# First projection of a hybrid decoder layer: a fixed row-by-row order, one low half on GpSimd, and VectorE's low parts as scalar_tensor_tensor

## The chip, the cores and the metric

The kernel runs on one core of a Trainium2 chip. The metric is the time of one execution in microseconds (us) on the device; lower is better. The core has five engines that run side by side, each working through its own list of instructions in order: TensorE (PE in the profile, with weight loads as PEld), VectorE (DVE), ScalarE (ACT), GpSimd (POOL) and SyncE (SP, which here only starts transfers). They meet through semaphores. Transfers between the memory outside (HBM) and the on-chip memory SBUF are done by 16 DMA engines.

## The reference, cut to what matters

One decoder layer with 256 tokens of width 2048. The part that the change touches is the beginning: a modulated RMS norm and the first projection.

```python
c_act = jax.nn.silu(c)
mod = (c_act @ w_ada[l] + b_ada[l]).reshape(B, 6, 1, D)
shift1, scale1, gate1, shift2, scale2, gate2 = jnp.moveaxis(mod, 1, 0)
h = rmsnorm(x, g_norm_mix[l]) * (1.0 + scale1) + shift1
q_a, k_c, v_c, k_s, v_s, k_w, v_w, g_a, q_r, k_r, v_r, g_r = split_cols(h @ w_in[l], IN_SIZES)
...
x = x + gate1 * (jnp.concatenate([o_nsa, o_ret], axis=-1) @ w_out[l])
h2 = rmsnorm(x, g_norm_ffn[l]) * (1.0 + scale2) + shift2
x = x + gate2 * peer_ffn(h2, peer_w_q[l], peer_sub_keys[l], peer_u[l], peer_v[l])
return rmsnorm(x, g_norm_final)
```

Everything is float32. Behind the projection come sparse attention, retention, the output projection and a retrieval over 16,384 experts; the change leaves them alone.

## The kernel before, in words

**Products in two parts.** TensorE multiplies in a shortened float32 format. To keep the precision, each operand is split: `hi` is the value rounded to that format (a cast on ScalarE), `lo` is the rest, `value - hi` (a subtraction on VectorE). A product is then three matmuls: hi·hi, hi·lo and lo·hi. `split` (L157, L158) makes `whi` and `wlo` of a weight tile `raw` (128 partitions x 2048 columns, 1,024 KB) in two halves of 1024 columns: cast, subtract, cast, subtract.

**The first projection, stage A.** It runs over eight rows k of `winA` (the first eight of the 16 blocks of 128 input features; 2048 output columns). Per row: SP starts the load of `winA[k]` (L348); `split` makes its parts; `row_in(k)` makes the activations of the block with `modulate`: ScalarE scales and shifts the block of `xT` (L295) and casts it to `hh` (L296), VectorE writes the low part `hl` (L297; `hh` and `hl` are the two halves of the tile `act`); TensorE runs 48 matmuls of 128x256 into eight PSUM banks, `bkA` (L354): first hi·hi for the first block of each bank, then the rest, bank by bank.

**Scales and shifts row by row.** The scale and shift of a block come from two rows of `w_ada`, which is read alongside as 128x2048 tiles, `adaT`. `ada_chunk` (L198) multiplies such a tile with the row `crow` and adds up over the columns, one VectorE instruction of 128x2048 and a small one that reads the accumulator out. `background` takes these tiles off a list; a row of stage A takes two (scale and shift of the next row) and then writes `modc` (L338) and `scol` (L339), which ScalarE needs for the next row's L295. So a row loads three tiles of 1,024 KB: one `winA`, two `adaT`.

**Buffers.** The raw tiles rotate through four buffers. SP starts loads in the order of the code, and a load waits until its buffer's last reader is done. `whi` and `wlo` have two buffers each.

**Before and behind stage A.** Ahead of it the squares of `xT` are summed, GpSimd raises the mean to the power -1/2 (L221), TensorE spreads it over the partitions, ScalarE copies it out (`rrow`, L275), and VectorE multiplies `xT` with it in four instructions (L300). Behind it the eight banks are copied out to `oT`, by VectorE and ScalarE in turn (L370, L372, `wait_in`), and stage C follows with four tiles `winC` of the same shape into the banks `bkC`, then stage B with 16 rows of `winB` (832 KB each).

**What sets the order.** The order on each engine is chosen by a scheduler from an estimate of times; only what is passed to `tc.keep_in_program_order` stays in the order of the code among such instructions of its engine. In stage A nothing was held in this way.

Of the kernel before, what the change touches and what calls it, by code (L numbers as in the profile page):

```python
# [9 lines left out]
F32 = mybir.dt.float32  # L10
F32R = mybir.dt.float32r
# [5 lines left out]
AF = mybir.ActivationFunctionType  # L17
OP = mybir.AluOpType
# [97 lines left out]
def body(ctx, tc, a, out, dbg=None, stop=None):  # L116
    nc = tc.nc
# [15 lines left out]
    def chunk_tile(name, dt, tag=None):  # L133
        pool, bufs = strm[-1]
        return pool.tile([P, 2048], dt, name=name, tag=tag or name, bufs=bufs[tag or name])
# [10 lines left out]
    def load(src):  # L146
        r = raw_tile()
        i = nc.sync.dma_start(r, src)
        if ring:
            tc.keep_in_program_order(i)  # L150
        return r

    def split_to(r, hi, lo, parts=1):
        n = hi.shape[-1] // parts
        for i in range(parts):
            sl = slice(i * n, i * n + n)
            nc.scalar.copy(hi[:, sl], r[:, sl])  # L157
            nc.vector.tensor_sub(lo[:, sl], r[:, sl], hi[:, sl].bitcast(F32))  # L158

    def split(r, n=2048, parts=2):  # L160
        hi, lo = chunk_tile("whi", F32R)[:, 0:n], chunk_tile("wlo", F32R)[:, 0:n]
        split_to(r[:, 0:n], hi, lo, parts)
        return hi, lo
# [4 lines left out]
    xT = base.tile([P, KB, S], F32, name="xT")  # L168
# [3 lines left out]
    b_col = cols[:, 0:96].rearrange("p (j k) -> p j k", k=KB)  # L172
    g_mix, g_ffn = cols[:, 96:112], cols[:, 112:128]
# [3 lines left out]
    modc = base.tile([P, 6, KB], F32, name="modc")  # L177
    scol = base.tile([P, 2, KB], F32, name="scol")
    def c_row(pool, psum=None, dst=None):

        r = pool.tile([P, D], F32, name="crow") if dst is None else dst
        if psum is None:
            nc.sync.dma_start(r, bass.AP(tensor=a["c"].tensor, offset=a["c"].offset, ap=[[0, P], [1, D]]))
            nc.scalar.activation(r, r, AF.Silu)
            return r
        c1 = raw_tile()[0:1, :]
        nc.sync.dma_start(c1, a["c"])
        for q in range(4):
            sl = slice(q * 512, (q + 1) * 512)
            ps = psum.tile([P, 512], F32, name="psc_", tag="A")  # L190
            nc.tensor.matmul(ps, ones[0:1, :], c1[:, sl], start=True, stop=True)
            nc.scalar.activation(r[:, sl], ps, AF.Silu)
        return r

    def ada_chunk(j, k, crow):

        r = load(a["adaT"][j, k])
        nc.vector.scalar_tensor_tensor(r, r, 1.0, crow, op0=OP.mult, op1=OP.mult, accum_out=modc[:, j, k:k + 1])  # L198

    def gate_store(j, ps, ident, t):  # L200

# [24 lines left out]
    hh, hl = act[:, :, 0, :], act[:, :, 1, :]  # L226
# [52 lines left out]
    with ExitStack() as fctx:  # L279
# [12 lines left out]
        def modulate(k, e, t, gi, sh, hh, hl):  # L292

            for i in range(k, e):
                nc.scalar.activation(t[:, i - k, :], t[:, i - k, :], AF.Identity, bias=modc[:, sh, i:i + 1], scale=scol[:, gi, i:i + 1])  # L295
            nc.scalar.copy(hh[:, k:e, :], t)  # L296
            nc.vector.tensor_sub(hl[:, k:e, :], t, hh[:, k:e, :].bitcast(F32))  # L297
# [14 lines left out]
        crow = c_row(fp, pp)  # L312
# [11 lines left out]
        todo = [(j, k) for k in range(KB) for j in (1, 0)] + [(j, k) for j in (2, 4, 3) for k in range(KB)] + [(5, k) for k in range(LATE)]  # L324

        credit = [0.0]

        def background(n=1):
            credit[0] += PACE[n] if isinstance(n, str) else n
            n = int(credit[0] + 1e-6)  # L330
            credit[0] -= n
            for _ in range(n):
                if not todo:
                    return
                j, k = todo.pop(0)
                ada_chunk(j, k, crow)
                if j == 0:
                    nc.vector.tensor_add(modc[:, 0:2, k], modc[:, 0:2, k], b_col[:, 0:2, k])  # L338
                    nc.vector.tensor_scalar(scol[:, 0, k:k + 1], modc[:, 1, k:k + 1], 1.0, g_mix[:, k:k + 1],  # L339
                                            op0=OP.add, op1=OP.mult)  # L340
                elif 1 < j < 5 and k == KB - 1:
                    nc.vector.tensor_add(modc[:, j, :], modc[:, j, :], b_col[:, j, :])
                    if j == 4:
                        nc.vector.scalar_tensor_tensor(scol[:, 1, :], modc[:, 4, :], 1.0, g_ffn, op0=OP.add, op1=OP.mult)

        def win_row(src, k, n):
            r = raw_tile()
            nc.sync.dma_start(r[:, 0:n], src[k])  # L348
            return split(r, n)

        def rows_T(bank, b, hi, lo, col, k, k0, k1, first=True):
            w = slice(col, col + P)
            for n, (x, y) in enumerate(((hi, hh), (hi, hl), (lo, hh))):
                nc.tensor.matmul(bank[:, b, :], x[:, w], y[:, k, :], start=k == k0 and n == 0 and first,  # L354
                                 stop=k == k1 - 1 and n == 2, skip_group_check=True)
# [6 lines left out]
        def row_in(k):  # L362
            while len(todo) > 80 + LATE - 2 * (k + 1):
                background(1)
            modulate(k, k + 1, xT[:, k:k + 1, :], 0, 0, hh, hl)

        def wait_in(dst, bk):
            for i, b in enumerate(bk):
                if i % 2:
                    nc.vector.tensor_copy(dst[:, 2 * i:2 * i + 2, :], b)  # L370
                else:
                    nc.scalar.copy(dst[:, 2 * i:2 * i + 2, :], b)  # L372

        background(2)
        bk = banks("bkA", [P, 2, S], "AASSTTOO")
        for k in range(KH):
            hi, lo = win_row(a["winA"], k, 2048)
            row_in(k)
            background("A")
            for b in range(16):  # L380
                rows_T(bk[b // 2], b % 2, hi, lo, b * P, k, 0, KH, b % 2 == 0)
        wait_in(oT, bk)
        bk = banks("bkC", [P, 2, S], "AASS")
        for q in range(KH // 2):
            hi, lo = split(load(a["winC"][q].rearrange("p k e -> p (k e)")))
# [8 lines left out]
        for k in range(KB):  # L394
            hi, lo = win_row(a["winB"], k, NB)
# [80 lines left out]
        for kv in range(2):  # L476
# [9 lines left out]
            for pb in range(16):  # L486
                i = nc.tensor.matmul(psc, w1[:, pb * P:(pb + 1) * P], blk[:, pb], start=pb == 0, stop=pb == 15)
# [34 lines left out]
        for gp in range(2):  # L522
# [3 lines left out]
            for r in range(4):  # L526
# [5 lines left out]
                for hf in range(2):  # L532
# [5 lines left out]
                    for br in range(2):  # L538
# [6 lines left out]
                        for tt, sl in ((0, slice(0, 128)), (1, slice(128, 384))):  # L545
# [3 lines left out]
                                                 accum_out=den[:, hf, tt, br:br + 1])  # L549
# [155 lines left out]
        for q in range(4):  # L705
            sl = slice(q * 512, (q + 1) * 512)
# [9 lines left out]
            with tc.high_priority(offset=100 if q == 3 else 0):  # L716
                for tt in range(2):
                    t = fp.tile([P, 512], F32, name="xg", tag="tmp2", bufs=3)
# [8 lines left out]
        for q in range(4):  # L727
            sl = slice(q * 512, (q + 1) * 512)
# [3 lines left out]
        for k in range(KB):  # L732
            with tc.high_priority(offset=(KB - k) * 10):
# [3 lines left out]
                t = xT[:, k, :]  # L737
# [9 lines left out]
    with ExitStack() as gctx:  # L747
# [49 lines left out]
        pin = tc.keep_in_program_order  # L797
# [544 lines left out]
def build(tc, a, out, dbg=None):  # L1342
    with ExitStack() as ctx:
        body(ctx, tc, a, out, dbg)
# [17 lines left out]
```

## Time and profile before

| | us |
|---|---|
| three runs, median | 1861.81 (1858.59 to 1864.34) |
| the profiled execution | 1856.91 |
| its span, first to last instruction | 1855.2 |
| TensorE busy in the span | 1793.1 (97%) |
| VectorE busy | 1485.7 (80%) |
| ScalarE busy | 708.7 (38%) |
| GpSimd busy | 366.1 (20%) |

How to read the lines that the prediction quotes. In the chain of waits a piece has its start and length in us and then what the time went to: an engine's line and tile, or a transfer. In the windows a line is a stretch of the span with each engine's busy time and its number of instructions. A row of the timeline has start, length, engine, line, operation, the tiles written and read, their shapes, the number of merged instructions, and in brackets how long the engine had been idle and what ended the wait. A row of a group of instructions has the busy time in us and the mean of one in ns. "adaT multiply" stands for L198, "low half" for L158 on 1024 columns.

### The profile page before, as it was taken

Reading aid. Unit: us, or ns where it says so; the run is one execution under the profiler, and the core shown is the slowest. Engines: PE = TensorE matmul, PEld = TensorE weight load, DVE = VectorE, ACT = ScalarE, POOL = GpSimd, SP = SyncE. Lnnn points to the kernel's source line nnn. Section 1 sums busy time; section 2 is a strip of 40 time slices with the busy share of each in tenths; the row PEclk is TensorE's granted clock in tenths of the full one; section 3 lists DMA queues with packets and bytes.
Section 4 is the critical chain, followed back from the end, with each engine's and each line's share of the span. In section 5 each row is a group of like instructions: output and inputs, shape, how many; then the busy total and the mean of one; then the engine's idle time right before and its main releaser. Section 6 shows DMA issues by size and latency. Waiting matters only on the chain.

```text
span 1855.2 us, 28510 instructions
## 1 busy us (share of the span) xinstructions
PE 1793.1 (97%) x11264; PEld 1571.5 (85%) x11264; DVE 1485.7 (80%) x2336; ACT 708.7 (38%) x1284; POOL 366.1 (20%) x259
## 2 busy tenths in 40 slices
PE   5899999999889999999999999999999999999997
PEld 4899878797767899999997777779999998777775
DVE  7988889889779999586498999983555558998878
ACT  3444453745435421021045555541111114555554
POOL 1000001011010012211124434420111114544210
PEclk9999899999999999999999999999999999999999
DMA  8989887889887799999889999989999989999992
GB/s 341 409 320 362 313 308 292 342 302 334 318 338 279 278 322 364 424 366 376 332 346 386 423 420 416 409 355 425 367 345 359 354 316 404 426 421 403 388 316 99
DMA packets 94616, 653.96 MB, mean 353 GB/s; under 512 B 11409, under 2 KB 11633, under 8 KB 18449
## 3 DMA queue, kind: packets, MB, share of 16 engines
q1 hardware_dynamic: 66818, 467.78, 65.2%
q0 software_dynamic: 27664, 184.37, 25.3%
q8 instruction: 88, 1.44, 0.3%
q14 instruction: 46, 0.38, 0.1%
HBM read 644.97 MB, written 4.22 MB: 350 GB/s over the span
## 4 chain that ended last, share of the span: by engine, by line
PE 87%; DVE 7%; DMA 3%; issue 1%; ACT 1%; POOL 0%; SPq 0%; ACTq 0%; POOLq 0%; DVEq 0%
PE acc L990 31%; PE psU L1111 28%; PE psN L453 8%; PE psD L354 4%; PE psA L237 3%; PE bkB L354 2%; DMA raw<-in_adaT 2%; PE psA L238 1%; PE pg L1096 1%; DVE raw L198 1%; DVE wlo L158 1%; PE bkC L354 1%; PE bvB L406 1%; DMA raw<-in_winA 1%; PE pT L552 1%
## 5 line engine op out<-in xcount | busy, mean ns | idle before, releaser
L1111 PE MATMUL psU<-xT,raw 128*128 128x160 f32 x4096 | 569.5, 300 | 0.0
L1111 PEld LDWEIGHTS psU<-xT,raw 128*128 128x128 f32 x4096 | 558.3, 190 | 0.4
L990 PE MATMUL acc<-whi,cc 128*128 128x512 f32 x1512 | 369.1, 391 | 0.0
L990 PEld LDWEIGHTS acc<-whi,cc 128*128 128x128 f32 x1512 | 283.8, 188 | 70.0 <-issue 1.5
L967 DVE TENSOR_TENSOR wlo<-raw,whi 128x2048 fp32r<-128x2048 f32 x126 | 288.1, 2287 | 55.1 <-issue 47.4
L990 PE MATMUL acc<-wlo,cc 128*128 128x512 f32 x1008 | 254.2, 392 | 0.8 <-DVE wlo L967 0.6
L964 ACT CAST whi<-raw 128x2048 fp32r<-128x2048 f32 x126 | 240.7, 1911 | 0.5 <-DMA raw<-in_v 0.5
L198 DVE SCALAR_TENSOR_TENSOR raw<-raw,crow 128x2048 f32<-128x2048 f32 x96 | 219.0, 2283 | 19.7 <-DMA raw<-in_adaT 19.6
L157 ACT CAST whi<-raw 128x1024 fp32r<-128x1024 f32 (+1 forms) x174 | 168.5, 1018 | 167.1 <-DMA raw<-in_winA 32.4
L158 DVE TENSOR_TENSOR wlo<-raw,whi 128x1024 fp32r<-128x1024 f32 (+1 forms) x174 | 200.6, 1181 | 24.2 <-ACT whi L157 23.8
L990 PEld LDWEIGHTS acc<-wlo,cc 128*128 128x128 f32 x1008 | 161.5, 161 | 63.8 <-DVE wlo L967 3.1
L453 PE MATMUL psN<-whi,act 128*128 128x512 f32 x512 | 166.9, 402 | 1.4 <-ACT act L677 0.7
L1117 DVE TENSOR_TENSOR X<-X,ge 128x160 f32<-128x160 f32 (+19 forms) x94 | 25.8, 276 | 162.7 <-ACT ge L1116 160.5
L1113 ACT ACTIVATE X<-psU 128x160 f32<-128x160 f32 (+19 forms) x102 | 25.6, 251 | 315.6 <-PE psU L1111 299.6
L453 PEld LDWEIGHTS psN<-whi,act 128*128 128x128 f32 x512 | 95.9, 189 | 25.6 <-issue 1.7
L453 PE MATMUL psN<-wlo,act 128*128 128x512 f32 x256 | 103.3, 404 | 3.4 <-DVE wlo L158 3.4
L953 ACT CAST cc<-X 128x192 fp32r<-128x192 f32 x126 | 44.0, 352 | 148.1 <-PE acc L990 147.5
L237 PE MATMUL psA<-act,whi 128*128 128x512 f32 x240 | 87.2, 404 | 3.8 <-ACT whi L157 3.8
L806 POOL DMA_INDIRECT rows<-in_urow,sx x32 | 67.1, 2097 | 105.3 <-DVE rows L847 100.4
L806 POOL DMA_INDIRECT s<-in_urow,sx x26 | 53.9, 2072 | 120.6 <-DVE s L847 86.5
L354 PE MATMUL psD<-act,whi 128*128 128x256 f32 x384 | 75.4, 294 | 0.6 <-ACT whi L157 0.6
L969 ACT CAST cc<-cc 128x64 fp32r<-128x64 f32 x126 | 30.4, 243 | 117.2 <-DVE cc L954 117.2
(363 smaller groups left out, 2551.0 us busy)
## 6 DMA issues: line engine op xcount, KB each, us to landing
raw<-in_u SPq DMA_DIRECT2D x128, 1024.0 KB
raw<-in_v SPq DMA_DIRECT2D x128, 1024.0 KB
raw<-in_adaT SPq DMA_DIRECT2D x96, 1024.0 KB
raw<-in_winN SPq DMA_DIRECT2D x16, 1024.0 KB
raw<-in_woutN SPq DMA_DIRECT2D x16, 1024.0 KB
raw<-in_wqT SPq DMA_DIRECT2D x16, 1024.0 KB
raw<-in_winB SPq DMA_DIRECT2D x16, 832.0 KB
raw<-in_winD SPq DMA_DIRECT2D x12, 1024.0 KB
```

Of the source, the lines that this page charges most:

```text
L157: nc.scalar.copy(hi[:, sl], r[:, sl])
L158: nc.vector.tensor_sub(lo[:, sl], r[:, sl], hi[:, sl].bitcast(F32))
L198: nc.vector.scalar_tensor_tensor(r, r, 1.0, crow, op0=OP.mult, op1=OP.mult, accum_out=modc[:, j, k:k + 1])
L237: nc.tensor.matmul(p_, hi[:, sl], act[:, k], start=k == 0, stop=False, skip_group_check=True)
L354: nc.tensor.matmul(bank[:, b, :], x[:, w], y[:, k, :], start=k == k0 and n == 0 and first, stop=k == k1 - 1 and n == 2, skip_group_check=True)
L453: nc.tensor.matmul(ps[tt], x[:, k, ts_], y[:, w], start=k == 0 and j == 0, stop=k == KB - 1 and j == 2)
L806: pin(nc.gpsimd.indirect_dma_start(out=r, out_offset=None, in_=src, in_offset=bass.IndirectOffsetOnAxis(ap=o, axis=0)))
L953: inorder(nc.scalar.copy(ch, xb(j)))
L964: inorder(nc.scalar.copy(hi, r))
L967: nc.vector.tensor_sub(lo[:, i:i + n], r[:, i:i + n], hi[:, i:i + n].bitcast(F32))
L990: return nc.tensor.matmul(acc[c][0:m], x, w[:, c[1] * 512:(c[1] + 1) * 512], start=jj == 0 and n == 0, stop=jj == HALF - 1 and n == 2 - c[ ...
L1111: nc.tensor.matmul(ps, w[:, k * P:(k + 1) * P], xT[:, k, 0:TU], start=k == 0, stop=k == KB - 1)
```

## The change

In stage A alone (a flag, `pinned`, is set ahead of its loop and cleared behind it):

- Every instruction of a row on ScalarE, VectorE and GpSimd is held in the order of the code, row by row: casts and low halves of the weights, activation, its cast and its low part, then the two adaT multiplies of the next row with `modc` and `scol`.
- The second low half of each `winA` tile is subtracted on GpSimd (L367 of the new code), the first one stays on VectorE.
- VectorE's subtractions of the stage (first low half and low part of the activations, both L353) are written as `scalar_tensor_tensor`, (x * 1.0) - y, in place of `tensor_sub`.

```diff
     def ada_chunk(j, k, crow):
 
         r = load(a["adaT"][j, k])
-        nc.vector.scalar_tensor_tensor(r, r, 1.0, crow, op0=OP.mult, op1=OP.mult, accum_out=modc[:, j, k:k + 1])
+        return nc.vector.scalar_tensor_tensor(r, r, 1.0, crow, op0=OP.mult, op1=OP.mult, accum_out=modc[:, j, k:k + 1])
...
         credit = [0.0]
+        pinned = [False]
+
+        def pin(i):
+            return tc.keep_in_program_order(i) if pinned[0] else i
...
                 j, k = todo.pop(0)
-                ada_chunk(j, k, crow)
+                pin(ada_chunk(j, k, crow))
                 if j == 0:
-                    nc.vector.tensor_add(modc[:, 0:2, k], modc[:, 0:2, k], b_col[:, 0:2, k])
-                    nc.vector.tensor_scalar(scol[:, 0, k:k + 1], modc[:, 1, k:k + 1], 1.0, g_mix[:, k:k + 1],
-                                            op0=OP.add, op1=OP.mult)
+                    pin(nc.vector.tensor_add(modc[:, 0:2, k], modc[:, 0:2, k], b_col[:, 0:2, k]))
+                    pin(nc.vector.tensor_scalar(scol[:, 0, k:k + 1], modc[:, 1, k:k + 1], 1.0, g_mix[:, k:k + 1],
+                                                op0=OP.add, op1=OP.mult))
...
+        def minus(dst, x, y):
+            if pinned[0]:
+                pin(nc.vector.scalar_tensor_tensor(dst, x, 1.0, y, op0=OP.mult, op1=OP.subtract))
+            else:
+                nc.vector.tensor_sub(dst, x, y)
+
         def win_row(src, k, n):
             r = raw_tile()
             nc.sync.dma_start(r[:, 0:n], src[k])
-            return split(r, n)
+            if not pinned[0]:
+                return split(r, n)
+            hi, lo = chunk_tile("whi", F32R)[:, 0:n], chunk_tile("wlo", F32R)[:, 0:n]
+            for i in range(2):
+                sl = slice(i * n // 2, (i + 1) * n // 2)
+                pin(nc.scalar.copy(hi[:, sl], r[:, sl]))
+                if i:
+                    pin(nc.gpsimd.tensor_sub(lo[:, sl], r[:, sl], hi[:, sl].bitcast(F32)))
+                else:
+                    minus(lo[:, sl], r[:, sl], hi[:, sl].bitcast(F32))
+            return hi, lo
...
         def row_in(k):
             while len(todo) > 80 + LATE - 2 * (k + 1):
                 background(1)
-            modulate(k, k + 1, xT[:, k:k + 1, :], 0, 0, hh, hl)
+            t = xT[:, k:k + 1, :]
+            pin(nc.scalar.activation(t[:, 0, :], t[:, 0, :], AF.Identity, bias=modc[:, 0, k:k + 1], scale=scol[:, 0, k:k + 1]))
+            pin(nc.scalar.copy(hh[:, k:k + 1, :], t))
+            minus(hl[:, k:k + 1, :], t, hh[:, k:k + 1, :].bitcast(F32))
...
         bk = banks("bkA", [P, 2, S], "AASSTTOO")
+        pinned[0] = True
         for k in range(KH):
             hi, lo = win_row(a["winA"], k, 2048)
             row_in(k)
             background("A")
             for b in range(16):
                 rows_T(bk[b // 2], b % 2, hi, lo, b * P, k, 0, KH, b % 2 == 0)
+        pinned[0] = False
```

What it does to the order. On VectorE, from the end of the norm's small instructions to row 1 (`wlo<-raw,whi` are low halves, `xT<-xT,rrow` is the normalisation, `act<-xT,act` the low part of the activations, `raw,modc<-raw,crow` an adaT multiply) the kernel before has:

```order
L269 TENSOR_SCALAR rdiag<-small,rcol 128x128 x2
L158 TENSOR_TENSOR wlo<-raw,whi 128x1024 x2
L300 TENSOR_TENSOR xT<-xT,rrow 128x1024 x4
L198 SCALAR_TENSOR_TENSOR raw,modc<-raw,crow 128x2048
L297 TENSOR_TENSOR act<-xT,act 128x256
L198 SCALAR_TENSOR_TENSOR raw,modc<-raw,crow 128x2048
L158 TENSOR_TENSOR wlo<-raw,whi 128x1024
L338 TENSOR_TENSOR modc<-modc,cols 128x2
L158 TENSOR_TENSOR wlo<-raw,whi 128x1024
L198 SCALAR_TENSOR_TENSOR raw,modc<-raw,crow 128x2048
L339 TENSOR_SCALAR scol<-modc,cols 128x1
L198 SCALAR_TENSOR_TENSOR raw,modc<-raw,crow 128x2048
```

and the changed kernel, on the same engine at the same place:

```order
L269 TENSOR_SCALAR rdiag<-small,rcol 128x128 x2
L300 TENSOR_TENSOR xT<-xT,rrow 128x1024 x4
L353 SCALAR_TENSOR_TENSOR wlo<-raw,whi 128x1024
L353 SCALAR_TENSOR_TENSOR act<-xT,act 128x256
L198 SCALAR_TENSOR_TENSOR raw,modc<-raw,crow 128x2048 x2
L343 TENSOR_TENSOR modc<-modc,cols 128x2
L344 TENSOR_SCALAR scol<-modc,cols 128x1
L353 SCALAR_TENSOR_TENSOR wlo<-raw,whi 128x1024
L353 SCALAR_TENSOR_TENSOR act<-xT,act 128x256
L198 SCALAR_TENSOR_TENSOR raw,modc<-raw,crow 128x2048 x2
```

Row 0's low halves stood ahead of the normalisation and one of them now stands behind it; the low part of the activations now stands ahead of both adaT multiplies of the next row, where before one of them, or in row 1 both, came first.

On GpSimd, behind the power operation of the first norm, the changed kernel has the eight subtractions, where before the transfers of the attention stage (`kT`, `nal`) followed at once:

```order
L551 MEMSET ppad_2371 128x512
L316 DMA rowc<-crow 16x1x128
L221 ISA
L221 TENSOR_TENSOR rcol<-rcol,mhalf 128x2
L367 TENSOR_TENSOR wlo<-raw,whi 128x1024 x8
L444 DMA kT_1730<-kcv 64x4x128 x4
L563 DMA nal<-in_nali 128x384 x9
```

Nothing on GpSimd but these eight is new.

On ScalarE, at the edge from stage A to stage C (`oT<-bkA` copies a bank out, `whi<-raw` is now the cast of a `winC` tile), the kernel before has:

```order
L372 COPY oT<-bkA_192 128x512
L372 COPY oT<-bkA_194 128x512
L157 CAST whi<-raw 128x1024 x2
L372 COPY oT<-bkA_196 128x512
L295 ACTIVATE xT<-xT,modc,scol 128x256
L372 COPY oT<-bkA_198 128x512
```

and the changed kernel:

```order
L396 COPY oT<-bkA_192 128x512
L396 COPY oT<-bkA_194 128x512
L396 COPY oT<-bkA_196 128x512
L396 COPY oT<-bkA_198 128x512
L157 CAST whi<-raw 128x1024 x2
L387 ACTIVATE xT<-xT,modc,scol 128x256
```

All four of ScalarE's bank copies now come ahead of the first cast of stage C. From there on the engines' lists hold the same instructions in the same order but for one adaT multiply and its neighbours on VectorE; SP's list of loads is the same throughout.

## The prediction, made before the result was known

> **What bounds the kernel now.** I read the chain of waits first, around the stage that the change touches (the first projection's eight rows, about 24 to 90 us). Start and length in us, then what:
>
> ```profile
> 72.23 7.27 DMA raw<-in_winA
> ...
> 79.57 1.06 ACT whi L157
> ...
> 80.66 2.36 DVE wlo L158 x2
> 83.02 2.21 DVE raw L198 x2
> 85.23 0.35 DVE act L297
> ...
> 85.62 5.00 PE bkA L354 x40
> 90.62 22.77 PE bkC L354 x192
> ```
>
> A row is a loop: winA's transfer, ScalarE's cast to the high half, VectorE's low halves, an adaT multiply, VectorE's low part of the activations (L297, "alo" below), and TensorE's last 40 matmuls of the row. From row 7's alo on the chain is TensorE alone. The table of windows (us, busy of PE, PEld, DVE, ACT, POOL, then clock, DMA share, GB/s) says how full each engine is:
>
> ```profile
> 65.00:70.00 5.00, 3.20 (x28) 3.00 (x26) 4.92 (x6) 1.91 (x4) 0.00 (x0) 1.00 1.00 415
> 75.00:80.00 5.00, 4.99 (x43) 4.79 (x42) 4.93 (x7) 0.43 (x1) 0.00 (x0) 1.00 0.99 411
> 85.00:90.00 5.00, 4.38 (x37) 4.38 (x38) 4.69 (x10) 2.88 (x4) 0.00 (x0) 1.00 1.03 431
> 90.00:140.00 50.00, 50.00 (x392) 48.49 (x391) 40.90 (x48) 23.51 (x33) 0.00 (x0) 1.00 0.89 326
> 140.00:186.00 46.00, 46.00 (x333) 43.35 (x332) 38.42 (x49) 19.88 (x30) 0.17 (x1) 1.00 0.95 363
> ```
>
> In the rows VectorE and the transfers are both full (4.9 of 5 us, share 1.0). A row moves three tiles of 1,024 KB, 3.15 MB: 7.7 us at 411 GB/s, 7.3 at the best window's 431. So taking work from VectorE alone can save at most some 0.4 us a row. From 90 to 186 us TensorE is busy without a gap: whatever row 7 gains or loses is carried on.
>
> VectorE's timeline, row 2's alo and then row 7:
>
> ```profile
> 46.11 0.42 DVE L297 TENSOR_TENSOR act<-xT,act 128x256 fp32r<-128x256 f32 x1
> ...
> 79.71 0.16 DVE L338 TENSOR_TENSOR modc<-modc,cols 128x2 f32<-128x2 f32 x1
> 79.91 0.21 DVE L339 TENSOR_SCALAR scol<-modc,cols 128x1 f32<-128x1 f32 x1
> 80.66 2.36 DVE L158 TENSOR_TENSOR wlo<-raw,whi 128x1024 fp32r<-128x1024 f32 x2 [0.54 <-ACT whi L157]
> 82.94 2.28 DVE L198 SCALAR_TENSOR_TENSOR raw<-raw,crow 128x2048 f32<-128x2048 f32 x1
> ...
> 85.14 0.42 DVE L297 TENSOR_TENSOR act<-xT,act 128x256 fp32r<-128x256 f32 x1
> 85.48 2.29 DVE L198 SCALAR_TENSOR_TENSOR raw<-raw,crow 128x2048 f32<-128x2048 f32 x1
> 87.69 0.08 DVE L198 DVE_READ_ACCUMULATOR raw<-raw,crow 128x1 f32 x1
> ```
>
> Start to start, a row costs VectorE 2.28 (two low halves, 1.14 each) + 2.20 + 0.34 (alo) + 2.21 + about 0.5 (accumulator, L338, L339) = 7.5 us. Alo of row 2 to alo of row 7 is 39.03 us, 7.81 a row.
>
> **The change part by part.** *The other form.* The page has both forms at one width:
>
> ```profile
> L967 DVE TENSOR_TENSOR wlo<-raw,whi 128x2048 fp32r<-128x2048 f32 x126 | 288.1, 2287 | 55.1 <-issue 47.4
> L198 DVE SCALAR_TENSOR_TENSOR raw<-raw,crow 128x2048 f32<-128x2048 f32 x96 | 219.0, 2283 | 19.7 <-DMA raw<-in_adaT 19.6
> ```
>
> 2,287 against 2,283 ns: the rewriting as scalar_tensor_tensor costs and saves nothing in itself.
>
> *The half that moves.* VectorE loses 1.14 us a row: 6.40 are left. GpSimd gains eight subtractions of 128x1024, of which it has none now; its nearest rows are fills:
>
> ```profile
> 2.58 0.19 POOL L470 MEMSET Kc<- 128x64 f32 x1
> 2.66 0.99 POOL L472 MEMSET BD<- 128x1024 f32 x1
> ```
>
> 960 more columns cost 0.80 us, 0.83 ns a column for one stream. A subtraction reads two streams and writes one: 0.99 if all three ran together, 0.14 + 2 x 0.85 = 1.84 if the reads take turns, 0.1 + 3 x 0.85 = 2.65 if all do. I take X = 2.24, the middle of the last two; one stream's fill is no model for three. The Trainium skill ("GPSIMD Engine Reference", section "Elementwise — side-by-side cycle accounting") has 4,497 ns for 2,048 columns, by which an estimate for 1,024 is 2.25 and the sum would be the same; no run here shows it.
>
> *Do the two engines get in each other's way?* GpSimd's power operation shows one direction:
>
> ```profile
> 311.71 4.91 POOL L221 TENSOR_TENSOR msn<-msn,mhalf 128x16 f32<-128x16 f32 x1 [23.07 <-DVE msn L611]
> 399.15 2.92 POOL L221 TENSOR_TENSOR msn<-msn,mhalf 128x16 f32<-128x16 f32 x1 [2.66 <-DVE brs L663]
> ...
> 311.54 2.28 DVE L198 SCALAR_TENSOR_TENSOR raw<-raw,crow 128x2048 f32<-128x2048 f32 x1
> ...
> 313.75 0.68 DVE L435 TENSOR_TENSOR xT<-oT,psD 128x512 f32<-128x512 f32 x1
> 314.35 2.35 DVE L158 TENSOR_TENSOR wlo<-raw,whi 128x1024 fp32r<-128x1024 f32 x2
> ...
> 449.68 2.35 DVE L158 TENSOR_TENSOR wlo<-raw,whi 128x1024 fp32r<-128x1024 f32 x2
> ...
> 449.87 1.58 POOL L221 TENSOR_TENSOR brs<-brs,mhalf 128x2 f32<-128x2 f32 x1 [2.51 <-DVE bnb L665]
> ```
>
> The same 128x16 operation takes 2.92 us at one place and 4.91 at another, where it was started inside an adaT multiply that went on for 2.04 us (to 313.75): 2.04 + 2.87. So a VectorE instruction with two SBUF inputs holds GpSimd off until it ends, in the scalar_tensor_tensor form too. At 449.87 the small one gets in between two back-to-back low halves, not behind both (0.95 to the first one's end, then 0.63). Does GpSimd hold VectorE off as well? The pair at 314.35 keeps its 2.35 us while the power operation runs, but that reads 16 columns and can be done reading by then. A subtraction reads 1,024 columns through most of its length, so I take it that VectorE's two-input instructions wait for it whole. The Trainium skill ("SBUF — State Buffer", section "SBUF: two separate sides") calls this an exclusive lock that whichever starts first keeps for its whole instruction; the trace agrees for VectorE as the first, and for GpSimd as the first it contradicts "whole" (the pair at 314.35 ran inside the 4.91 us). By the rule word for word the sum below is the same; by the row, read as "VectorE is never held", it is the first rival's.
>
> Nearly all of VectorE's work in a row has two SBUF inputs, so GpSimd's 2.24 is then added to VectorE's 6.40: 8.64 us a row, above the 7.7 of the transfers. The start:
>
> ```profile
> 20.61 1.99 ACT L157 CAST whi<-raw 128x1024 fp32r<-128x1024 f32 x2 [6.44 <-DMA raw<-in_winA]
> 23.91 0.37 ACT L275 COPY rrow<-psr 128x256 f32<-128x256 f32 x1 [1.31 <-PE psr L271]
> 28.01 1.99 ACT L157 CAST whi<-raw 128x1024 fp32r<-128x1024 f32 x2 [0.93 <-DMA raw<-in_winA]
> ...
> 24.79 4.63 DVE L300 TENSOR_TENSOR xT<-xT,rrow 128x1024 f32<-128x1024 f32 x4
> ```
>
> The casts of row 0 now stand behind the copy of rrow, row 0's low halves behind the normalisation. VectorE begins that at 24.3 and needs 4.6 us; ScalarE's casts of rows 0 and 1 are done by 26.2 and 30, so both GpSimd subtractions wedge in before row 1's alo. Alo of row 1: 24.3 + 4.6 + 2X + row 0's (1.14 + 0.34 + 4.42 + 0.5) + row 1's 1.48 = 36.8 + 2X = 41.3. Six more rows of 6.40 + X: alo of row 7 ends at 75.2 + 8X = **93.1**, against 85.48 now: **+7.6**. With X = 1.84 it is +4.4, with 2.65 +10.9; with 0.99 the transfers bind again.
>
> *Waits that are added.* SP's adaT load of row k+2 goes into row k's winA buffer and now waits for GpSimd too, with two more loads queued behind it on SP; but GpSimd is done ahead of alo, so this binds only at the start: row 0's buffer was free by 24.8, now about 34.5. winA of row 2 is then issued about 39.3 and wanted by ScalarE about 45; with the 7.27 us of the chain it is 1.5 late at worst, with an emptier queue not at all. I take 0, and keep 1.5 for the range. TensorE's upper banks wait for GpSimd's half, which is there 1.5 us ahead of alo.
>
> *The edge to the next stage.* The fourth copy of bkA now stands ahead of the next weights' cast on ScalarE:
>
> ```profile
> 88.19 1.99 ACT L157 CAST whi<-raw 128x1024 fp32r<-128x1024 f32 x2
> 90.09 0.58 ACT L372 COPY oT<-bkA 128x512 f32<-128x512 f32 x1
> ...
> 90.46 1.11 PE L354 MATMUL bkC<-act,whi 128*128 128x256 f32 x8
> ```
>
> Now the cast was begun 2.3 us before TensorE needed it. Then it starts after the copy of the last bank but one, which TensorE leaves 0.6 us before its end E: copy done about E + 0.1, half a cast (1.05) later TensorE may start, E + 1.25, and VectorE's low half comes 0.2 after the eight matmuls that cover it: **+1.4**, where nothing was lost.
>
> Sum: 7.6 + 1.4 = **+9.0 us**. The profiled execution took 1856.91 us (span 1855.2), so 1865.9 on its scale; it lies 4.9 under the median of the three runs, 1861.81, and the change will be timed like those: **1870.8**. The edits behind 90 us are none, and TensorE has no gap to take the delay up before 186.
>
> **The rivals.** *GpSimd never holds VectorE* (not slower). For it: the pair at 314.35 undisturbed. Against it: a short read proves little, and the other direction is a clean hold. It decides from the point where VectorE's wait on a subtraction is under 1.3 us a row (7.7 less 6.40), since then the transfers bind. winA of row 7 lands at 79.50 as now; casts to 81.6, activation and its cast about 0.95 more, alo 0.34: 82.9, that is -2.6, and +1.4 at the edge: -1.2, 1860.6. If the transfers run at 431 GB/s throughout, five rows save 2.2 more: -3.4, 1858.4.
>
> *X at 1.84 or less with holding both ways*: +4.4 + 1.4 = +5.8 at 1.84, down to the first rival below 1.3.
>
> *The rewritten form frees the port*, so that only adaT multiplies collide: alo and the low half (1.48 a row) run beside GpSimd, at most 8 x 1.48 = 11.8 less, and the transfers bind: again the first rival's time. The 2.04 us hold by that very form speaks against it.
>
> **How the numbers follow.** Held both ways 0.68 (of that four fifths over +5.6), never held 0.24, something between or small X 0.04, a gain from later waits of TensorE for transfers that fall better 0.04. A measurement of this kernel can tell about 0.3%, 5.6 us, from no change. Slower: 0.53; within: 0.41; faster: 0.06. The range reaches from the first rival's 1858.4 to 10.9 + 1.4 + 1.5 over the median, 1875.6: 1858 to 1876. The likeliest case's own range is 1867 to 1876.
>
> **What would show it.** Alo of row 7 at 93 (right) or 83 (first rival); rows 8.6 or 7.7 us apart; adaT multiplies or low halves of VectorE longer than 2.29 and 1.22 us, or gaps before them while GpSimd works; GpSimd's subtractions near 2.2 us, or longer by a VectorE instruction; a gap of TensorE of 1 to 1.5 us ahead of the first bkC. Wrong would make it a GpSimd subtraction under 1.5 us, or transfers that run far off 7.7 us a row.

## The result and the profile after

| | before | changed |
|---|---|---|
| median of five runs each, us | 1859.76 (1858.59 to 1864.34) | 1872.78 (1866.52 to 1875.28) |
| ratio | | 1.0066 [1.0053, 1.008] |
| the profiled execution, us | 1856.91 | 1866.52 |
| its span, us | 1855.2 | 1864.3 |
| VectorE busy, us | 1485.7 | 1492.0 |
| GpSimd busy, us | 366.1 | 388.5 |

The change makes the kernel slower by 0.66%, 12.3 us on the median of before; the two medians are 13.0 apart. A second measurement of the same changed kernel (the last experiment but one) gave 1.0054 [1.0035, 1.0073], 10.0 us. Forecast was +9.0, to 1870.8 us, and the two profiles differ by 9.1 in the span and 9.6 in the time. One run of the kernel before in the second group of experiments (4648.85 us) and one of the kernel with the mended edge and no GpSimd half (4611.69 us) took about 2.5 times as long as all others and are left out of the medians and ratios below. VectorE is busy for 6.3 us more although eight subtractions of 1.14 us were taken from it: that is the first sign of where the time went.

The chain of waits of the changed kernel in stage A (start, length in us, what):

```profile
26.39 4.53 DVE xT L300 x2
30.91 3.28 DVE wlo L353
...
45.39 8.56 DMA raw<-in_winA
...
84.33 4.51 DVE raw L198 x4
88.84 0.02 issue
88.86 2.31 DVE modc L343
...
92.86 2.29 DVE raw L198 x2
...
101.02 22.04 PE bkC L375 x184
```

VectorE carries most of the chain up to 101 us (two transfers of winA stand in it besides), where before TensorE took over for good at 85.6. Two steps stand out: a low half of 3.28 us, where such an instruction took 1.22, and `modc`, an addition of 128x2, that took 2.31 us in place of 0.16. The timeline shows both beside GpSimd (start, length, engine, line, operation, tiles and shapes, idle time before):

```profile
29.88 3.24 POOL L367 TENSOR_TENSOR wlo<-raw,whi 128x1024 fp32r<-128x1024 f32 x1 [1.18 <-ACT whi L365]
47.66 2.41 POOL L367 TENSOR_TENSOR wlo<-raw,whi 128x1024 fp32r<-128x1024 f32 x1 [14.55 <-PE bkA L375]
...
63.84 3.25 POOL L367 TENSOR_TENSOR wlo<-raw,whi 128x1024 fp32r<-128x1024 f32 x1 [5.25 <-PE bkA L375]
...
88.76 2.39 POOL L367 TENSOR_TENSOR wlo<-raw,whi 128x1024 fp32r<-128x1024 f32 x1 [4.63 <-ACT whi L365]
...
30.84 3.36 DVE L353 SCALAR_TENSOR_TENSOR wlo<-raw,whi 128x1024 fp32r<-128x1024 f32 x1
...
40.85 2.29 DVE L198 SCALAR_TENSOR_TENSOR raw<-raw,crow 128x2048 f32<-128x2048 f32 x1
...
46.62 1.23 DVE L353 SCALAR_TENSOR_TENSOR wlo<-raw,whi 128x1024 fp32r<-128x1024 f32 x1 [0.81 <-ACT whi L365]
48.50 1.85 DVE L353 SCALAR_TENSOR_TENSOR act<-xT,act 128x256 fp32r<-128x256 f32 x1 [0.66 <-ACT act L388]
50.27 2.28 DVE L198 SCALAR_TENSOR_TENSOR raw<-raw,crow 128x2048 f32<-128x2048 f32 x1
...
64.85 2.53 DVE L353 SCALAR_TENSOR_TENSOR act<-xT,act 128x256 fp32r<-128x256 f32 x1
...
88.86 2.30 DVE L343 TENSOR_TENSOR modc<-modc,cols 128x2 f32<-128x2 f32 x1
...
92.86 2.28 DVE L198 SCALAR_TENSOR_TENSOR raw<-raw,crow 128x2048 f32<-128x2048 f32 x1
```

Read the ends, not the lengths. GpSimd's subtraction of row 7 runs from 88.76 to 91.15, and `modc`, begun at 88.86, ends at 91.16. In row 2 the subtraction ends at 50.07 and alo, begun at 48.50, at 50.35; in row 4 the subtraction ends at 67.09 and alo, begun at 64.85 with no idle time before it, at 67.38. In these two rows 0.28 and 0.29 us, the rest of alo's own work, come behind the subtraction. VectorE's instruction is recorded as busy while it stands and waits for GpSimd's to end. The next adaT multiply starts where alo is done, so its start gives the rows' pace: 40.85 (row 1), 50.27 (row 2), 92.86 (row 7): 9.42 us for one row, then five of 8.52, against 7.81 before.

The groups of instructions from 20 to 105 us have the sum of it (count, busy us, mean ns):

```profile
L367 POOL TENSOR_TENSOR wlo<-raw,whi 128x1024 fp32r<-128x1024 f32 x8 | 22.0, 2749 | 47.3 <-ACT whi L365 27.5 <-PE bkA L375 19.8
L353 DVE SCALAR_TENSOR_TENSOR act<-xT,act 128x256 fp32r<-128x256 f32 x8 | 12.0, 1501 | 1.8 <-ACT act L388 1.8
```

Alo has a mean of 1,501 ns, against 0.42 us for one that nothing holds. The subtractions took 2.39 to 2.41 us where they were begun within the last 0.2 us of a VectorE instruction, and up to 3.25 where they were begun earlier inside one. From the end of VectorE's low half to their own end it was 2.21 to 2.23 us in all of rows 2 to 6.

The windows (PE, PEld, DVE, ACT, POOL busy, then clock, DMA share, GB/s) answer to those of before:

```profile
90.00:140.00 50.00, 46.96 (x374) 45.48 (x373) 43.20 (x52) 23.44 (x32) 1.14 (x1) 1.00 0.88 320
140.00:186.00 46.00, 46.00 (x334) 43.34 (x333) 39.50 (x48) 20.43 (x28) 0.00 (x0) 1.00 0.95 364
```

TensorE was busy for all of 90 to 140 us before and now idles 3.04 of it. From 140 to 186 it is full as before, so nothing is made up there. At the edge, PE and ACT in the timeline:

```profile
94.38 0.59 ACT L396 COPY oT<-bkA 128x512 f32<-128x512 f32 x1 [1.90 <-PE bkA L375]
97.93 0.59 ACT L396 COPY oT<-bkA 128x512 f32<-128x512 f32 x1 [0.35 <-PE bkA L375]
98.41 2.00 ACT L157 CAST whi<-raw 128x1024 fp32r<-128x1024 f32 x2
...
99.51 1.21 PE L375 MATMUL bkC<-act,whi 128*128 128x256 f32 x8 [1.03 <-ACT whi L157]
101.02 0.38 PE L375 MATMUL bkC<-act,wlo 128*128 128x256 f32 x1 [0.30 <-DVE wlo L158]
```

The cast comes behind the fourth copy, and TensorE waits 1.03 us for the first half of it and 0.30 us for the low half.

### The profile page after: what moved, and what is told of

Same layout as the page of the kernel before. It is cut to its first block, busy times and chain, and to the rows that moved or that the text cites. A ratio compares the mean times of both kernels' runs of the same rounds, so it can differ in the third digit from the quotient of the medians.

```text
span 1864.3 us, 28535 instructions
## 1 busy us (share of the span) xinstructions
PE 1795.8 (96%) x11264; PEld 1573.0 (84%) x11264; DVE 1492.0 (80%) x2328; ACT 710.2 (38%) x1284; POOL 388.5 (21%) x267
## 4 chain that ended last, share of the span: by engine, by line
PE 83%; DVE 10%; DMA 3%; issue 2%; ACT 1%; POOL 0%; SPq 0%; ACTq 0%; POOLq 0%; DVEq 0%
PE acc L1016 30%; PE psU L1137 28%; PE psN L479 7%; PE psA L237 3%; PE bkB L375 2%; DVE raw L198 2%; PE psD L375 2%; DMA raw<-in_adaT 2%; DVE wlo L158 2%; PE psA L238 1%; PE pg L1122 1%; PE bvB L432 1%; PE bkC L375 1%; DMA raw<-in_winA 1%; PE sc L568 1%
## 5 line engine op out<-in xcount | busy, mean ns | idle before, releaser
L157 ACT CAST whi<-raw 128x1024 fp32r<-128x1024 f32 (+1 forms) x158 | 152.6, 1016 | 138.8 <-PE psN L479 25.4
L158 DVE TENSOR_TENSOR wlo<-raw,whi 128x1024 fp32r<-128x1024 f32 (+1 forms) x158 | 182.7, 1183 | 25.8 <-ACT whi L157 25.4
L832 POOL DMA_INDIRECT rows<-in_v,sx x25 | 63.4, 2534 | 57.0 <-DVE sp L879 31.0
```

Source lines behind the costliest of these rows:

```text
L832: pin(nc.gpsimd.indirect_dma_start(out=r, out_offset=None, in_=src, in_offset=bass.IndirectOffsetOnAxis(ap=o, axis=0)))
```

## The experiments

The kernels were run in three groups, each beside runs of the kernel before on the same chip: 1860.14 us (median of 23), 1860.47 (25) and 1859.07 (17).

**The GpSimd half taken back.** Order and form stay.

```diff
                 if i:
-                    pin(nc.gpsimd.tensor_sub(lo[:, sl], r[:, sl], hi[:, sl].bitcast(F32)))
+                    minus(lo[:, sl], r[:, sl], hi[:, sl].bitcast(F32))
```

> The change with its order and its form kept, but both low halves on VectorE and none on GpSimd. If the wait of VectorE's two-input instructions for GpSimd's subtraction is the cost, VectorE needs 7.5 us a row, the transfers bind again at about 7.7 us a row, alo of row 7 ends near 83 us, the gap of TensorE ahead of the first bkC stays at about 1.3 us, and the span is 1854.5 us, give or take 2 (the kernel before 1855.2, the change 1864.3); timed within 0.3% of the kernel before. Rival, the fixed order is the cost: the span stays at 1861 or more and the time 0.3% or more over the kernel before.

Measured: 1861.64 us, ratio 1.0013 [0.9999, 1.0028]; span 1859.3. VectorE in row 7, and TensorE's first waits of stage C:

```profile
84.10 2.35 DVE L353 SCALAR_TENSOR_TENSOR wlo<-raw,whi 128x1024 fp32r<-128x1024 f32 x2
86.37 0.42 DVE L353 SCALAR_TENSOR_TENSOR act<-xT,act 128x256 fp32r<-128x256 f32 x1
...
93.29 1.21 PE L375 MATMUL bkC<-act,whi 128*128 128x256 f32 x8 [1.45 <-ACT whi L157]
95.11 0.39 PE L375 MATMUL bkC<-act,wlo 128*128 128x256 f32 x1 [0.62 <-DVE wlo L158]
```

Alo ends at 86.7, 6.2 us ahead of the change's, and no instruction of VectorE is stretched: most of the cost is the GpSimd half, and what order and form cost together is at most 0.28%, by the interval. The wait at the edge is there without GpSimd, as expected of an effect of the copies, but it is 1.45 + 0.62 = 2.07 us where about 1.3 was expected. The span was missed too (1859.3, expected at 1854.5 give or take 2), and so was the place of alo: expected to end near 83, it ended at 86.7. Row 1's alo ended at 38.72, from where six rows of 7.5 us would give 83.7; most of the rest is waits of VectorE for ScalarE's casts, 2.1 us in three rows (0.81, 0.47 and 0.82).

**The form undone.** The change with `tensor_sub` on VectorE in place of the scalar_tensor_tensor.

```diff
-                pin(nc.vector.scalar_tensor_tensor(dst, x, 1.0, y, op0=OP.mult, op1=OP.subtract))
+                pin(nc.vector.tensor_sub(dst, x, y))
```

> The change with VectorE's subtractions of the stage as tensor_sub again, the second half still on GpSimd. If the form does nothing: rows of 8.5 us, alo of row 7 near 92.9 us, span 1864 us give or take 2, time 0.5 to 0.8% over the kernel before, as the change. Rival, the scalar_tensor_tensor form spares the port at least in part: VectorE's instructions that start inside a GpSimd subtraction are held longer, and the span is 3 us or more over the change's.

Measured: 1871.77 us, ratio 1.0067 [1.0048, 1.0087], as the change's 1.0066. Row 7's alo in this form:

```profile
91.31 2.22 DVE L353 TENSOR_TENSOR act<-xT,act 128x256 fp32r<-128x256 f32 x1 [0.29 <-ACT act L388]
```

It is held like the other form (2.22 for 0.42 us), and the next multiply starts at 93.45, against 92.86. So the form does nothing that shows. The span, 1870.6, lies outside the expected 1862 to 1866 and 6.3 over the change's, which is what the rival asked for; but the attention stage's first power operation starts at 321.91, 0.5 us later than in the change (321.38), so nearly all of that is lost behind the stage.

**The order undone.** The GpSimd half and the form stay, and the scheduler orders the stage.

```diff
         def pin(i):
-            return tc.keep_in_program_order(i) if pinned[0] else i
+            return i
```

> Second half on GpSimd and the scalar_tensor_tensor form, but nothing held in the order of the code. If GpSimd's half is the cost: rows of about 8.5 us in most of the stage, alo of row 7 at 91 to 94 us, span 1861 to 1866 us. Rival, the fixed order is the cost: alo of row 7 at 83 to 86 us and the span within 2 us of the 1855.2 of the kernel before.

Measured: 1877.56 us, ratio 1.0096 [1.0077, 1.0115], the slowest of all. GpSimd in rows 4 and 5, ScalarE and VectorE in row 5:

```profile
67.00 2.41 POOL L367 TENSOR_TENSOR wlo<-raw,whi 128x1024 fp32r<-128x1024 f32 x1 [7.80 <-ACT whi L365]
77.21 2.41 POOL L367 TENSOR_TENSOR wlo<-raw,whi 128x1024 fp32r<-128x1024 f32 x1 [7.80 <-ACT whi L365]
...
74.59 0.60 ACT L387 ACTIVATE xT<-xT,modc,scol 128x256 f32<-128x256 f32 x1 [7.42 <-DVE scol L344]
75.10 1.98 ACT L365 CAST whi<-raw 128x1024 fp32r<-128x1024 f32 x2
...
77.42 2.48 DVE L353 SCALAR_TENSOR_TENSOR act<-xT,act 128x256 fp32r<-128x256 f32 x1
```

A row is 10.2 us. Here the activation, which waits 7.42 us for `scol` of VectorE, stands ahead of the casts, so adaT multiplies, activation, casts and subtraction follow one another. The next multiply behind row 7's alo starts at 100.24, where 91 to 94 was expected, and the span is 1874.8 in place of 1861 to 1866. The expectation had this kernel at or under the change, and it came out 0.3% above: with the GpSimd half in place the fixed order doesn't cost, it makes that half cheaper than the scheduler's order does.

**GpSimd writes without reading.** In place of the subtraction it fills its half with zeros, which leaves the products of that half's low part out.

```diff
-                    pin(nc.gpsimd.tensor_sub(lo[:, sl], r[:, sl], hi[:, sl].bitcast(F32)))
+                    pin(nc.gpsimd.memset(lo[:, sl].bitcast(F32), 0.0))
```

> GpSimd fills the second low half with zeros instead of subtracting (it leaves out the lo*hi products of half of the columns of the stage); a fill writes 128x1024 and reads nothing. If it is GpSimd's reading that holds VectorE: no instruction of VectorE in the stage is stretched (1.22, 0.42 and 2.28 us throughout), rows of 7.7 us, alo of row 7 near 83 us, span 1854.5 give or take 2. Rival, any GpSimd instruction on SBUF holds VectorE: instructions that start inside a fill last up to 0.9 us longer.

Measured: 1860.08 us, ratio 1.0008 [0.9995, 1.0021]; span 1856.2.

```profile
66.64 0.95 POOL L367 MEMSET wlo<- 128x1024 f32 x1 [6.36 <-PE bkA L375]
...
66.66 1.23 DVE L353 SCALAR_TENSOR_TENSOR wlo<-raw,whi 128x1024 fp32r<-128x1024 f32 x1 [0.80 <-ACT whi L365]
...
83.31 0.42 DVE L353 SCALAR_TENSOR_TENSOR act<-xT,act 128x256 fp32r<-128x256 f32 x1 [0.60 <-ACT act L388]
```

The low half and the fill run side by side at full pace, and so does every other instruction of VectorE with two inputs that meets a fill. With the work off VectorE and none of these held, the next multiply behind row 7's alo starts at 83.66, 1.8 us ahead of the kernel before, and the edge (1.04 + 0.30 us) takes most of it back. This is close to the first rival's case, which was put at alo 82.9 and -1.2 us; measured is no change that shows, and the interval's lower end, -0.9 us, falls just short of the rival's figure.

One instruction of VectorE was held by the fills all the same. The first two, of rows 0 and 1, run beside the norm's small instructions `rdiag` (L269), which scale one tile by a column of factors:

```profile
21.65 1.83 POOL L367 MEMSET wlo<- 128x1024 f32 x2
...
21.72 1.91 DVE L269 TENSOR_SCALAR rdiag<-small,rcol 128x128 f32<-128x128 f32 x2 [0.58 <-POOL rcol L221]
```

The pair takes 1.91 us in place of 0.48 and ends at 23.63, behind the fills' end at 23.48; the normalisation starts at 25.35, in the change at 24.11. So the rival of this expectation, that any GpSimd instruction holds VectorE, is true of this form with one tile as its input and false of the forms with two.

**One input instead of two.** GpSimd copies the weights into its half (the subtraction is left out).

```diff
-                    pin(nc.gpsimd.tensor_sub(lo[:, sl], r[:, sl], hi[:, sl].bitcast(F32)))
+                    pin(nc.gpsimd.tensor_copy(lo[:, sl], r[:, sl]))
```

> GpSimd copies the second half of the weight tile into the low half, with one input, instead of subtracting the high half (this leaves out the subtraction). If only a GpSimd instruction with two SBUF inputs holds VectorE, no VectorE instruction is stretched (1.22, 0.42 and 2.28 us throughout, as with the fill), the low part of row 7 is near 83.5 and the span near 1856. If every GpSimd instruction that reads SBUF in a stream holds it, VectorE's low parts are stretched beyond 1.5 us, the row is 6.4 plus the copy's length, and the low part of row 7 ends behind 86.

Measured: 1861.73 us, a single run; span 1859.9.

```profile
58.43 1.35 POOL L367 CAST wlo<-raw 128x1024 fp32r<-128x1024 f32 x1 [6.24 <-DMA raw<-in_winA]
...
58.92 0.87 DVE L343 TENSOR_TENSOR modc<-modc,cols 128x2 f32<-128x2 f32 x1
```

Neither expectation holds as it was written. `modc` is held, 0.87 us in place of 0.16, and ends at 59.79 with the copy (59.78): one input is enough to hold VectorE. But the copy is 1.03 us long where nothing delays it and no longer waits for the cast, so in rows 4 to 7 it falls on `modc` and not on the low parts (1.22 and 0.43 us throughout), and rows 3 to 7 take 7.5 us each: the next multiply behind row 7's alo starts at 83.9.

**A quarter instead of a half.** 512 columns of a winA tile on GpSimd, 1536 on VectorE.

```diff
-            for i in range(2):
-                sl = slice(i * n // 2, (i + 1) * n // 2)
+            for i, sl in enumerate((slice(0, 3 * n // 4), slice(3 * n // 4, n))):
```

> The change with 512 columns of each winA tile on GpSimd and 1536 on VectorE, in place of 1024 and 1024. If the hold lasts as long as the GpSimd subtraction, which goes with its columns (about 1.2 us for 512), a row is 6.40 + 0.57 + 1.2 = 8.2 us on VectorE and the low part of row 7 ends at 75.2 + 8 x 1.8 = 89.5, with a span about 3.4 under the change's. If the hold is a fixed price for each GpSimd instruction (2.2 us), the row is 9.2 and the low part of row 7 ends near 97.

Measured: 1867.42 us, ratio 1.0038 [1.0023, 1.0053]; span 1865.5. Row 7:

```profile
87.60 2.29 POOL L366 TENSOR_TENSOR wlo<-raw,whi 128x512 fp32r<-128x512 f32 x1 [6.07 <-ACT whi L364]
...
86.99 1.76 DVE L353 SCALAR_TENSOR_TENSOR wlo<-raw,whi 128x1536 fp32r<-128x1536 f32 x1 [0.30 <-ACT whi L364]
88.67 1.51 DVE L353 SCALAR_TENSOR_TENSOR act<-xT,act 128x256 fp32r<-128x256 f32 x1
```

GpSimd starts inside VectorE's low half, stands until that ends at 88.75, and works 1.14 us from there to 89.89; alo, begun at 88.67, ends at 90.18. Both directions of the hold are in these three rows, and the price goes with the columns: from the end of VectorE's low half the subtraction takes 1.14 us for 512 and 2.21 to 2.23 for 1024. Alo was expected at 89.5 and ended at 90.2. The ratio is lower than the change's two by 0.0028 and 0.0016, 5 and 3 us, though the interval overlaps with the second one's. The one span isn't lower (1865.5 against 1864.3, with an edge of 1.82 us in place of 1.33).

**The edge mended.** The change, with the first winC tile loaded, cast and split ahead of the last row's adaT multiplies, and the bank copies held behind it.

```diff
                 if i % 2:
-                    nc.vector.tensor_copy(dst[:, 2 * i:2 * i + 2, :], b)
+                    pin(nc.vector.tensor_copy(dst[:, 2 * i:2 * i + 2, :], b))
                 else:
-                    nc.scalar.copy(dst[:, 2 * i:2 * i + 2, :], b)
+                    pin(nc.scalar.copy(dst[:, 2 * i:2 * i + 2, :], b))
...
             row_in(k)
+            if k == KH - 1:
+                r0 = load(a["winC"][0].rearrange("p k e -> p (k e)"))
+                h0, l0 = chunk_tile("whi", F32R), chunk_tile("wlo", F32R)
+                for i in range(2):
+                    sl = slice(i * 1024, (i + 1) * 1024)
+                    pin(nc.scalar.copy(h0[:, sl], r0[:, sl]))
+                    minus(l0[:, sl], r0[:, sl], h0[:, sl].bitcast(F32))
             background("A")
...
-        pinned[0] = False
         wait_in(oT, bk)
+        pinned[0] = False
...
-            hi, lo = split(load(a["winC"][q].rearrange("p k e -> p (k e)")))
+            hi, lo = (h0, l0) if q == 0 else split(load(a["winC"][q].rearrange("p k e -> p (k e)")))
```

> The change with the edge from stage A to stage C put back: the first winC tile is loaded, cast (ScalarE) and split (VectorE) ahead of the adaT multiplies of the last row, and the copies of the banks stand behind it. If the wait of TensorE at the first bkC (1.33 us in the change) comes from the four bank copies that stand ahead of the cast, it goes to under 0.3 us, and a profile is about 1.3 us shorter than the change's 1864.3 at the same clock (1863); the low part of row 7's activations stays at about 92.9, since VectorE's work ahead of it is the same. If the wait has another cause (the transfer of winC, the copies themselves), it stays at about 1.3.

Measured: 1867.08 us, ratio 1.0038 [1.0026, 1.005]; span 1863.7. The only wait that TensorE has left near the edge:

```profile
100.92 0.50 PE L375 MATMUL bkC<-act,whi 128*128 128x256 f32 x2 [0.31 <-DVE oT L394]
```

The 1.33 us came from the copies ahead of the cast (in the change the cast starts as the fourth copy ends and waits for no transfer): with the cast at 91.94 they are gone, but for 0.31 us behind a copy of VectorE, and alo of row 7 starts at 90.15 and ends at 92.7, as in the change.

**The edge mended, no GpSimd half.** The same edit and both low halves on VectorE.

> The same edge, with both low halves on VectorE (no GpSimd half) and the fixed order and scalar_tensor_tensor kept. Low part of row 7 at 86.5 as in the run without the GpSimd half, the 2.07 us of wait at the first bkC gone: span about 1857.2 against that run's 1859.3, ratio to the kernel before between 0.999 and 1.001. If the two stage edges hang together (an earlier winC load takes the transfers' share from the adaT tiles), the wait turns up again later in stage C and the span stays near 1859.

Measured: 1858.52 us, ratio 0.9991 [0.998, 1.0002]; span 1856.8.

```profile
84.51 0.42 DVE L353 SCALAR_TENSOR_TENSOR act<-xT,act 128x256 fp32r<-128x256 f32 x1
...
93.33 0.50 PE L375 MATMUL bkC<-act,whi 128*128 128x256 f32 x2 [0.52 <-DVE oT L394]
```

The 2.07 us are gone but for 0.52, and alo comes at 84.5, 1.9 us ahead of the run without this edit though nothing differs up to there but the loads behind row 7's winA tile: I take that much for scatter of the transfers. The interval includes 1, so this kernel isn't shown to beat the one before.

This kernel and the one before it differ in the GpSimd half alone, so the two give its price by itself: the spans are 6.9 us apart (1863.7 and 1856.8), the ratios 0.47% (1.0038 and 0.9991, 8.7 us), and their intervals don't meet.

**The change again.** Nothing edited, for a second profile.

> The changed kernel as it is, once more, for a second profile. Its first profile took 1866.52 us, the lowest of five runs (median 1872.78). In stage A nothing should move: low part of row 7's activations at 92.9, rows of 8.5 us, 1.3 us of wait at the first bkC. If the missing 3 to 6 us lie in stage A, the subtractions or the rows are longer in this profile; if they lie later, the GpSimd power operation of the attention stage (321.38 in the first profile) starts within 1 us of that, and the time is lost between there and the last of the small power operations (557.27 in the first profile, 563.97 in the run with tensor_sub).

Measured: 1869.32 us, ratio 1.0054 [1.0035, 1.0073]; span 1866.4. Stage A is as before: alo of row 7 starts at 90.03 and ends at 92.5, the edge has its 1.03 us, and the power operation of the attention stage starts at 320.92 (321.38 in the first profile). What this execution took longer was lost behind that.

**Row 0 ahead of the normalisation.** The kernel with the mended edge and no GpSimd half, with row 0's casts and low halves left to the scheduler.

```diff
         for k in range(KH):
+            pinned[0] = k > 0
             hi, lo = win_row(a["winA"], k, 2048)
+            pinned[0] = True
```

> Both low halves on VectorE, the fixed order from row 1 on, the first winC tile cast and split ahead of the bank copies, and row 0's casts and low halves left to the scheduler, which puts them ahead of the normalisation as in the kernel before. If VectorE sets the rows' pace, the low part of row 7 comes 2.3 us earlier than with row 0 in the fixed order (84.9), at about 82.6, and the span is about 1854.5; if the transfers set it (7.3 to 7.7 us a row), it comes at 83.5 to 85 and the span stays at 1856 to 1857. Ratio to the kernel before 0.997 to 0.999.

Measured: 1858.69 us, ratio 1.0 [0.9988, 1.0012]; span 1857.8. Alo of row 7 ends at 83.4, between the two expectations, and the first power operation of the attention stage starts at 308.94, 2.8 us ahead of the kernel before. None of it reaches the end. More than that is lost again, 4 us of it between 463 and 552 us, where the chain of both kernels has two waits for adaT tiles (this one's has a third, of 6.97 us at 523.34); in this kernel:

```profile
466.68 6.60 DMA raw<-in_adaT
...
477.98 8.85 DMA raw<-in_adaT
```

in the kernel before:

```profile
468.20 4.87 DMA raw<-in_adaT
...
477.77 6.39 DMA raw<-in_adaT
```

and in the change with `tensor_sub`:

```profile
478.84 5.85 DMA raw<-in_adaT
...
489.39 10.05 DMA raw<-in_adaT
```

The two waits sum to 11.3 us before, 15.5 and 15.9 in the others: over 4 us come and go at this one place, with the GpSimd half and without it.

## Why the prediction was right, step by step

- **VectorE and the transfers both full, so that work taken from VectorE earns little.** Right, and shown from the other side: with GpSimd filling and not reading, VectorE is 1.14 us a row lighter and unheld in the rows, and alo of row 7 comes only 1.8 us earlier.
- **The form costs and saves nothing.** Right: 1.0067 with `tensor_sub`, 1.0066 without.
- **X, GpSimd's subtraction, 2.24 us.** Its recorded length is 2.39 to 2.41 where little delays it. Counted from the end of the VectorE instruction that it waits for, it is 2.21 to 2.23, and that is what VectorE then waits for. That 2.24 comes so close is luck in part: it was the middle of two guesses, 1.84 and 2.65.
- **Held both ways, whole, so a row is 6.40 + X = 8.64.** The mechanism is right and the row is 8.52. In row 4, where VectorE has no idle time, alo takes 2.45 us to the next multiply's start in place of 0.34: a hold of 2.11, and 6.40 + 2.11 is the row. That is 0.1 under the 2.2 us that GpSimd works, since alo needs only 0.29 of its 0.42 us once the subtraction has ended. In row 3 part of the same time is recorded as a wait for ScalarE (0.66) and the rest as a longer alo (1.85), and the row is the same 8.5. The Trainium skill ("SBUF — State Buffer", section "SBUF: two separate sides") has the pair of SBUF ports that VectorE and GpSimd share locked for the whole instruction by whichever starts first. For the subtraction the trace agrees to 0.01 us (91.15 and 91.16); the power operation, by which the prediction doubted "whole", is no model for a stream of 1,024 columns.
- **Row 1's alo at 41.3, row 7's at 93.1.** 40.85 and 92.86.
- **SP's wait, 0 with 1.5 kept.** Mis-sized: SP's adaT loads of row 2 went out at 34.27 (24.90 before), winA of row 2 at 38.98, VectorE waited 0.81 us for the cast of that tile, and row 2 is 0.9 longer than the others. That the last row came out within 0.3 of the forecast is the offset of this by rows that were 0.12 shorter and a start 0.4 earlier.
- **The edge, +1.4.** 1.33 (1.03 + 0.30), and gone when the cast stands ahead of the copies.
- **No gap to take the delay up.** Right up to the attention stage: its power operation starts at 321.38 against 311.71, 9.7 later, with the span 9.1 longer.
- **The first rival** (never held) falls on the stretched instructions, and the fill shows that its place of alo was about right (83.7 for 82.9). Its lower end is a little off: five rows at 431 GB/s in place of 411 save 1.8 us, not 2.2. **The form as the cure** falls too: scalar_tensor_tensor is held.

The forecast time came nearer than the forecast change, and that is luck: 1870.8 is 2.0 under the measured median, but +9.0 is 4.0 under the 13.0 between the medians. The three runs of before that it was counted from had their median at 1861.81, and with two more runs it is 1859.76.

Left open is the difference between +9.1 on one pair of profiles and +12.3 and +10.0 on the medians. The changed kernel reaches the attention stage's first power operation 9.7 and 9.2 us after the kernel before in its two profiles. From there to the last of the small power operations (548.43 before, 557.27 in the change) the twelve profiles take 235.9 to 242.3 us: 238.2 in the mean of the six whose GpSimd subtracts, 238.6 in that of the other six. So single executions differ there by some 6 us, and these profiles give no sign that a kernel that comes late loses more.

## What to carry to other kernels

Work handed from VectorE to GpSimd was not taken off VectorE here, where VectorE's instructions have two SBUF inputs and GpSimd's reads SBUF: a subtraction that took 1.14 us of VectorE's row took 2.1 us of it from GpSimd (8.52 less 6.40). Look for it in the ends: an instruction of VectorE that ends with GpSimd's and is far longer than its own kind is a wait, though it is counted as busy. And where an order is fixed for one stage, look at what it puts in front of the next stage's first instruction: here four copies cost 1.3 to 2.1 us.

## What was not expected of the hardware

- One input is enough: a GpSimd copy of 1,024 columns held a 128x2 addition of VectorE to its own end, 0.87 us in place of 0.16. A fill of the same size (0.95 us) held no two-input instruction of VectorE. For those the section of the Trainium skill named above limits the lock to GpSimd operations that read SBUF; both runs agree.
- A GpSimd instruction that reads nothing can hold VectorE all the same: two fills stretched the pair of `rdiag` instructions, which have one tile as their input, from 0.48 to 1.91 us. No run here shows why these are held and those with two inputs are not.
- The GpSimd copy takes 1.03 us, the subtraction 2.40, both as recorded: the second input costs more than the first and the write together.
